# Branch B's second half with GpSimd in a written order, weight sums tile by tile, and early loads of head 0

## The chip, the cores and the metric

The kernel runs on one core of a Trainium2 chip. Its engines are TensorE (PE: matmuls and transposes), VectorE (DVE), ScalarE (ACT), GpSimd (POOL) and SyncE (SP), which here issues every load and store. The metric is the time of one execution in microseconds (us); lower is better. TensorE's clock is granted by a throttle, and the profile lists it as a share of full speed.

## The reference

One encoder block over 1024 tokens of width 1024, with 16 meta tokens in front, in fp32: a norm, one wide projection `w_in`, two attention branches, two gates, and a feed-forward part.

```python
h = rms_norm(concat(meta, x), norm_mix)
proj = h @ w_in                    # qa ka va (512 each) | qb 512, kb vb 128 each | ga gb (1024 each)
# branch A: 4 heads of differential attention over all 1040 keys
s1 = q1 @ k1.T * scale - slope * dist ; s2 = q2 @ k2.T * scale - slope * dist
y_a = rms_norm((softmax(s1) - lam * softmax(s2)) @ v, subln_gain) * 0.8
# branch B: 8 heads (2 groups of 4, one key head each), a window of 128 tokens
# to either side, the meta tokens, and a sink in the divisor
y_b = softmax_with_sink(window(qb @ kb.T) * scale + bias) @ vb
x = x + (sigmoid(ga) * (y_a @ w_branch_a) + sigmoid(gb) * (y_b @ w_branch_b)) @ w_out
x = x + (silu(hn @ w_ff_gate) * (hn @ w_ff_up)) @ w_ff_down      # hn = rms_norm(x, norm_ffn)
out = rms_norm(x, norm_final)[meta dropped]
```

## The kernel before

**Precision.** Each fp32 operand is split into a high and a low half (`split`: ScalarE copies the high half, another engine subtracts it for the low half), and a product is three matmuls: high x high, low x high, high x low. `prep` loads a projection's 1024 x 128 columns (`w_c`), splits them into `wh_c` and `wl_c`, and leaves the low half to GpSimd but for one weight.

**Stages.** 1. The norm, the transposes of the tokens, projections. 2. Branch B's first group (`units_b(0)`) and heads 0 and 1 of branch A's projections. 3. `project_qb(1)`, the second group's queries; then `units_b(1)`, its eight tiles of 128 queries, and the projections of heads 2 and 3 (`project_a(2)`, `project_a(3)`), which send queries, keys and values to memory (`qa_d`, `ka_d`, `va_d`). A scheduler interleaves all of these on TensorE, by what is ready in a model of times; the other engines' order falls out of it. 4. The seam: pools of stage 3 are closed and others opened on their memory; head 0's queries, keys and values are loaded (`load_a`: `aq0_0`, `aq0_1`, `ak0_0`, `ak0_1`, `av0`), and the first gate products run. 5. Branch A, 4 heads x 8 tiles, where TensorE's order is written out by hand, with gate products as filler. 6. The branches' outputs (`ppa`), the merge, `w_out`, the feed-forward part.

**A tile of branch B** (`attend_b`): TensorE makes the scores `bps`, VectorE adds the bias and finds the extreme, ScalarE makes the exponentials, VectorE the reciprocal of the divisor `bdn`, GpSimd multiplies the four heads by it (`bs`) and copies the meta part (`bmd`). `finish`, one tile later, transposes on TensorE (`bpt`), splits (`btr`), multiplies with the values (`bpy`), and stores `yb_d`.

**The gates** are 2 x 8 column blocks, computed with Strassen's scheme of seven products for each 2 x 2 blocking (`order_g`, 56 products, named `pg2_0` for scheme number 2 and block 0). Each is four steps of three 512-column matmuls. Four of the seven need sums of weight blocks: `weight_sums(k)` loads raw blocks `gw` in two halves, makes four sums `gs` on GpSimd, and stores them to `ws_d`, from where `g_load` fetches them. `g_split` splits what was loaded. Products of numbers 1, 6 and 7 are added by VectorE to a kept partial result `gk` fetched again from `g_d`; the others are copied by ScalarE (`gate_stage`) and stored there. The token operand `hT_hi`, `hT_lo` is replaced by sums of tokens (`ts_d`, two loads of 1 MB) when the scheme's number demands it.

**Branch A's filler.** Each tile walks through a string of slots: `s` scores, `g` one gate step, `n` the tail of an earlier pair of tiles, `t` its transposes. Before head 0's first score `G_FIRST` = 28 gate steps run, before each other head `G_HEAD` = 10. `n_gates` is the budget of steps until the last tile: 4 x 56 - 36 = 188, where `HOLD` = 36 are kept for after it. 28, 10 before each of three heads, and five in a tile use it up by tile 26.

**SP** issues transfers in order: one that waits for data holds up those behind it.

Of the kernel before, what the change touches and what calls it, by code (L numbers as in the profile page):

```python
# [9 lines left out]
F32 = mybir.dt.float32  # L10
# [29 lines left out]
SLOTS = "sgsgsngsgsgstntnt"  # L40
SLOTS_LAST = "sgsgsngsgsstntnt"
# [6 lines left out]
HOLD = 36  # L48
# [3 lines left out]
G_FIRST = 28  # L52
# [21 lines left out]
def encoder_block(ctx: ExitStack, tc: tile.TileContext, x, meta, norm_mix, w_in, lq1, lk1, lq2, lk2,  # L74
# [30 lines left out]
    ws_d = {(p, k): dram.tile([P, 4, P], F32, name=f"ws_d{p}_{k}") for p in (5, 3, 6, 7) for k in range(8)}  # L105
# [68 lines left out]
    def prep(col, name, p=None, lo_eng=None):  # L174
        w = wpool.tile([P, DC, P], F32, tag="w", name=f"w_{name}", bufs=2)
        nc.sync.dma_start(w, w_in[:, col:col + P].rearrange("(c p) n -> p c n", p=P))
        p, bufs = (p, 1) if p else (wpool, W_BUFS)
        wh = p.tile([P, DC, P], F32R, tag="wh", name=f"wh_{name}", bufs=bufs)
        wl = p.tile([P, DC, P], F32R, tag="wl", name=f"wl_{name}", bufs=bufs)
        split(wh, wl, w, lo_eng or nc.gpsimd)  # L180
        return wh, wl

    order = [C_KB, C_QB, C_VB]
    for h in range(AH):
        order += [C_QA + h * P, C_VA + h * P, C_KA + h * P]
# [238 lines left out]
    prepped[C_QB + P] = prep(C_QB + P, "qbx", bpool, nc.vector)  # L424
# [129 lines left out]
    def units_b(g, qb, pending=()):  # L554
# [28 lines left out]
    def weight_sums(k):  # L583
        tt = nc.gpsimd.tensor_tensor
        for c in range(0, 4, 2):
            raw = tpool.tile([P, 2, 2, 256], F32, tag="to", name=f"gw_{k}_{c}", bufs=2)
            for kh in range(2):
                nc.sync.dma_start(raw[:, kh], g_weights(k, kh, 0, 256)[:, c:c + 2])
            a11, a21, a12, a22 = (raw[:, i, :, j * P:j * P + P] for i in range(2) for j in range(2))
            s1, s2, s3, s4 = (x[:, i] for x in [tpool.tile([P, 2, 2, P], F32, tag="ta", name=f"gs{j}_{k}_{c}", bufs=3)  # L590
                                                for j in range(2)] for i in range(2))
            tt(s1, a21, a22, ALU.add)
            tt(s3, a11, a21, ALU.subtract)
            tt(s2, s1, a11, ALU.subtract)
            tt(s4, a12, s2, ALU.subtract)
            for i, t in ((5, s1), (7, s3), (6, s2), (3, s4)):
                nc.sync.dma_start(ws_d[i, k][:, c:c + 2], t)
# [5 lines left out]
    def g_load(n, raw=None):  # L603
# [4 lines left out]
        nc.sync.dma_start(raw, ws_d[p, k] if (p, k) in ws_d else g_weights(k, *{2: (1, 0), 1: (0, 0), 4: (1, P)}[p], P))  # L608
# [26 lines left out]
    token_sums(3)  # L635
    qb = new_qb(1)
# [17 lines left out]
    def load_a(h, between=lambda: None):  # L654
        p = apool
        qs, ks = [None, None], [None, None]
        for m in (1, 0):
            q = qs[m] = p.tile([P, S], F32R, tag=f"q{m}", name=f"aq{h}_{m}")
            k = ks[m] = p.tile([P, 2, L], F32R, tag=f"k{m}", name=f"ak{h}_{m}")
            nc.sync.dma_start(f32(q), qa_d[h][m])  # L660
            nc.sync.dma_start(f32(k)[:, 0, :], ka_d[h][m])
            for hl in range(2):
                nc.sync.dma_start(f32(k)[64 - 64 * hl:128 - 64 * hl, 1, :], ka_d[h][m, 64 * hl:64 * hl + 64, :])
            if m:
                between()
        v = p.tile([P, 2, 9, P], F32R, tag="v", name=f"av{h}")
        nc.gpsimd.memset(f32(v)[:, 0, 8, :], 0.0)
        nc.sync.dma_start(f32(v)[:, :, 0:8, :], va_d[h][:, :, 0:8, :])
        nc.sync.dma_start(f32(v)[:2 * NM, 0, 8, :], va_d[h][:2 * NM, 0, 8, :])
        nc.sync.dma_start(f32(v)[2 * NM:3 * NM, 0, 8, :], va_d[h][:NM, 1, 8, :])  # L670
        return qs, ks, v

    project_a(2)
    project_a(3)
    for n in range(2):
        g_load(n, tpool.tile([P, 512], F32, tag="ta", name=f"w_g{n}", bufs=3))
        g_split(n, tpool.tile([P, 2, 4, P], F32R, tag="to", name=f"w_gop{n}", bufs=2))
    g_done[:] = [2, 2]
    ld = load_a(0, lambda: load_sums(5, 0, 1))
    flush_v()  # L680
# [4 lines left out]
    gpool, close_gpool = pool("gpool", "right")  # L685
    g_ahead(0)
# [17 lines left out]

    def gate_steps():
        for n, (p, k) in enumerate(order_g):
            g_ahead(n + 1)
            op, act = g_ready.pop((p, k)), G_ACT[p]
            if p in (2, 5, 1):
                g_bank[k] = pp_bank(f"pg{p}_{k}")  # L710
            ps = g_bank[k]
            for c in range(4):
                for i, (a, b) in enumerate(((0, 0), (0, 1), (1, 0))):
                    nc.tensor.matmul(ps, op[:, a, c], quad(b, *act)[:, c], start=(p in (2, 5, 1) and c == 0 and i == 0),  # L714
                                     stop=(p in (2, 3, 4) and c == 3 and i == 2), skip_group_check=True)
                if c == 3:
                    if p in (1, 6, 7):
                        st = g_kept.pop((p, k))
                        nc.vector.tensor_tensor(st, ps, st, ALU.add)
                    else:  # L720
                        st = gpool.tile([P, 512], F32, tag="g", name="gate_stage", bufs=G_BUFS)
                        nc.scalar.copy(st, ps)  # L722
                    nc.sync.dma_start(g_place(p, k), st)
                    if (p, k) in ((5, 3), (5, 7), (3, 7)):
                        later_p = {(5, 3): 6, (5, 7): 7, (3, 7): 4}[p, k]
                        load_sums(later_p, *G_ACT[later_p])
                yield
# [79 lines left out]
    gates = gate_steps()  # L807

# [639 lines left out]
```

## Time and profile before

| | |
|---|---|
| median of 3 runs | 1499.75 us (1498.25 to 1500.34) |
| the profiled execution | 1498.84 us |
| its span | 1496.9 us |
| TensorE busy in the span | 1439.3 us (96%) |
| GpSimd busy in the span | 667.6 us (45%) |
| VectorE busy in the span | 885.1 us (59%) |
| second group's queries begin | 178.2 us |
| first score of branch A | 365.85 us |
| first product of stage 6 | 670.13 us |

The span is that of the traced instructions in one execution; the execution's own time is 1.9 us longer. A line of the timeline gives the start, the busy time, the engine, the source line, the operation, what it writes and reads, shapes and count, and in square brackets how long the engine stood ahead of it and what released it. A line of the waits gives who waited for what, the sum, the number and the longest. A wait of TensorE counts in the time; one of another engine only where TensorE waits for it in turn.

### The profile page before, as it was taken

How to read it: one execution, taken by the hardware profiler on the slowest of the kernel's cores; microseconds unless marked ns; L12 is line 12 of the kernel's file. 1: busy time of each engine (PE TensorE's matmuls, PEld its weight loads, DVE VectorE, ACT ScalarE, POOL GpSimd, SP SyncE). 2: the span in 40 equal slices, each digit the busy share in tenths (PEclk: the TensorE clock that was granted, in tenths of full speed). 3: DMA queues.
4: the chain of work that ended last, by engine and by line, in shares of the span. 5: the costliest groups of instructions: out<-in, count | busy, mean ns of one | idle time of the engine just before them, and what ended most of it. 6: DMA issues, size and time to landing. Idle time of an engine off the chain costs nothing.

```text
span 1496.9 us, 21310 instructions
## 1 busy us (share of the span) xinstructions
PE 1439.3 (96%) x7279; PEld 1228.5 (82%) x7279; DVE 885.1 (59%) x1610; ACT 679.0 (45%) x1293; POOL 667.6 (45%) x622
## 2 busy tenths in 40 slices
PE   8999989996999999799999999999999999999997
PEld 6999868975989998778888878888888888788886
DVE  7478325541968787833440786655555554778566
ACT  6366425543655555635521573333333333344444
POOL 5599548523343443223732475545554443000344
PEclk9999999998999999999999999999999999999999
DMA  8366778549367747048640345333333333864443
GB/s 238 86 200 210 229 209 257 151 147 284 135 196 249 227 142 248 27 162 260 210 162 22 133 121 162 114 99 104 106 106 106 106 106 106 315 213 134 131 123 141
DMA packets 190204, 242.42 MB, mean 162 GB/s; under 512 B 19520, under 2 KB 117248, under 8 KB 190096
## 3 DMA queue, kind: packets, MB, share of 16 engines
q1 hardware_dynamic: 190096, 241.07, 51.0%
q8 instruction: 57, 0.93, 0.3%
q14 instruction: 51, 0.42, 0.1%
HBM read 157.45 MB, written 77.00 MB: 157 GB/s over the span
## 4 chain that ended last, share of the span: by engine, by line
PE 75%; DMA 7%; POOL 6%; issue 5%; DVE 3%; SPq 2%; ACT 2%; POOLq 0%; ACTq 0%; DVEq 0%
PE pg L1229 26%; PE pg L714 8%; PE pd L1323 8%; PE po L1006 5%; PE ppa L702 4%; PE aps L742 3%; PE pp_va L204 3%; POOL oa L118 3%; PE apy L781 3%; PE pp_qa L204 2%; PE apt L768 2%; PE pp_ka L204 2%; DMA ak<-ka_d 2%; PE bps L318 1%; PE bpt L343 1%
## 5 line engine op out<-in xcount | busy, mean ns | idle before, releaser
L118 POOL TENSOR_TENSOR wop<-wf,wop 128x512 fp32r<-128x512 f32 x128 | 172.4, 1351 | 164.7 <-ACT wop L117 152.3
L1229 PE MATMUL pg<-t,wop 128*128 128x512 f32 x1056 | 242.9, 389 | 0.2 <-POOL wop L118 0.2
L1229 PEld LDWEIGHTS pg<-t,wop 128*128 128x128 f32 x1056 | 198.2, 188 | 41.7 <-POOL wop L118 0.6
L1323 PE MATMUL pd<-ob,oa 128*128 128x512 f32 x924 | 210.2, 389 | 1.7 <-DVE ob L118 1.2
L1323 PEld LDWEIGHTS pd<-ob,oa 128*128 128x128 f32 x924 | 173.3, 188 | 38.4 <-DVE ob L118 1.7
L1229 PE MATMUL pg<-b,wop 128*128 128x512 f32 x792 | 184.0, 390 | 2.3 <-DVE c L1238 2.3
L1229 PEld LDWEIGHTS pg<-b,wop 128*128 128x128 f32 x792 | 148.3, 188 | 33.7 <-issue 2.4
L714 PE MATMUL pg<-hT_hi,gop 128*128 128x512 f32 x432 | 159.9, 399 | 12.9 <-ACT gate_stage L722 12.0
L118 POOL TENSOR_TENSOR gop<-gr,gop 128x512 fp32r<-128x512 f32 x54 | 72.1, 1336 | 151.9 <-ACT gop L117 146.5
L118 POOL TENSOR_TENSOR oa<-ra,oa 128x512 fp32r<-128x512 f32 x33 | 44.0, 1336 | 171.6 <-ACT oa L117 170.2
L117 ACT ACTIVATE wop<-wf 128x512 fp32r<-128x512 f32 x128 | 80.1, 631 | 84.3 <-PE pg L1229 48.5
L714 PEld LDWEIGHTS pg<-hT_hi,gop 128*128 128x128 f32 x432 | 82.1, 190 | 27.4 <-ACT gate_stage L722 12.7
L117 ACT ACTIVATE oa<-ra 128x512 fp32r<-128x512 f32 x77 | 48.7, 632 | 108.2 <-PE pd L1323 53.4
L742 PE MATMUL aps<-ak,aq 128*128 128x392 f32 (+1 forms) x384 | 92.0, 329 | 2.4 <-DVE at L772 0.7
L750 ACT ACTIVATE as<-as,amn 128x1040 f32<-128x1040 f32 x64 | 74.4, 1163 | 37.2 <-DVE amn L745 34.5
L1006 PE MATMUL po<-woh,mT 128*128 128x512 f32 x384 | 88.0, 390 | 0.0
L1064 DVE TENSOR_TENSOR s<-wf,wf 128x512 f32<-128x512 f32 x22 | 25.2, 1145 | 105.9 <-DMA wf<-in_w_ff_gate_dram 58.0
L714 PE MATMUL pg<-hT_lo,gop 128*128 128x512 f32 x216 | 86.0, 398 | 0.0
L1006 PEld LDWEIGHTS po<-woh,mT 128*128 128x128 f32 x384 | 71.9, 188 | 14.8
L742 PEld LDWEIGHTS aps<-ak,aq 128*128 128x128 f32 x384 | 68.7, 188 | 17.6 <-DVE amn L745 2.1
L745 DVE CUSTOM_DVE_ANT_0 as<-aps,dist,far_a 128x392 f32<-128x392 f32 x64 | 39.6, 619 | 51.8 <-PE aps L742 51.1
L320 DVE CUSTOM_DVE_ANT_0 bs<-bps,tbx,nsink 128x432 f32<-128x432 f32 (+1 forms) x64 | 38.1, 623 | 50.4 <-PE bps L318 38.2
(279 smaller groups left out, 3100.8 us busy)
## 6 DMA issues: line engine op xcount, KB each, us to landing
ra<-aop SPq DMA_DIRECT2D x77, 256.0 KB, 2.7
wf<-in_w_ff_gate_dram SPq DMA_DIRECT2D x24, 512.0 KB, 3.9
wf<-in_w_ff_up_dram SPq DMA_DIRECT2D x24, 512.0 KB, 3.8
aop<-as SPq DMA_DIRECT2D x44, 256.0 KB, 2.1
w_c<-in_w_in_dram SPq DMA_DIRECT2D x17, 512.0 KB, 5.8
aop<-c SPq DMA_DIRECT2D x33, 256.0 KB, 2.0
ts_d<-to SPq DMA_DIRECT2D x16, 512.0 KB, 3.9
gw<-in_w_in_dram SPq DMA_DIRECT2D x32, 256.0 KB, 4.2
```

The costliest lines, as they stand in the source:

```text
L117: nc.scalar.activation(hi, src, AF.Copy)
L118: lo_eng.tensor_tensor(lo, src, f32(hi), ALU.subtract)
L204: nc.tensor.matmul(ps[:, :n], a[:, c, :], b[:, c, at:at + n], start=(c == 0 and i == 0), stop=(c == DC - 1 and i == 2))
L702: nc.tensor.matmul(ps, w[:, a, j, :], src(j, b, tk), start=(j == 0 and n == 0), stop=(j == 3 and n == 2))
L714: nc.tensor.matmul(ps, op[:, a, c], quad(b, *act)[:, c], start=(p in (2, 5, 1) and c == 0 and i == 0), stop=(p in (2, 3, 4) and c == 3 and ...
L742: nc.tensor.matmul(ps[:, :n], qs[m][:, t * P:(t + 1) * P], ks[m][:, vv, k0:k0 + n], start=(vv == 0), stop=(vv == 1))
L745: nc.vector.tensor_tensor_reduce(s[m][:, k0:k0 + n], ps[:, :n], far_by, slope, low, ALU.add, ALU.min, mn[:, m, i:i + 1])
L750: nc.scalar.activation(s[m][:, 0:L], s[m][:, 0:L], AF.Exp, bias=low, scale=-1.0, accum_out=dn[:, m:m + 1])
L781: nc.tensor.matmul(py[:, cols], v[:kp, a, k, :], at_[:kp, k, b, :], start=(k == 0 and j == 0), stop=(k == 8))
L1006: nc.tensor.matmul(ps, mT[:, c, a, t * P:(t + 1) * P], wos[q, c][:, b], start=(c == 0 and n == 0), stop=(c == DC - 1 and n == 2))
L1229: nc.tensor.matmul(ps, op[:, x, c, :], b[:, y, c, :], start=(p in (1, 2, 5) and c == 0 and n == 0), stop=(p in (4, 2, 3) and c == 3 and n ...
L1323: nc.tensor.matmul(ps[u], oa[:, a, u * P:(u + 1) * P], ob[:, b, :], start=(p in (1, 2, 5) and j == 0 and k == 0), stop=(p in (2, 3, 4) and ...
```

## The change

It has five parts.

1. The low halves of the query weights of branch B's second group and of all projections of heads 2 and 3 are made by VectorE (`on_vector`), no longer by GpSimd.
2. From `project_qb(1)` to `flush_v()` GpSimd's instructions stand in the order in which they are written (`manual_schedule`). Each tile's `bs` and `bmd` come first, then the tile's two half blocks of weight sums (`sums_of`), whose loads are issued two halves ahead. Two sums go to memory in one store of 256 KB where there were two of 128 KB (`ws_d[k]`).
3. A new pool, `lowpool`, has memory that comes free when branch B's first group is done. `aq0_1`, `ak0_1` and `ak0_0` lie in it and are loaded at the start of stage 3 (`load_a1`, `load_k`). At the seam only `aq0_0` and `av0` are left (`load_a0`).
4. Four gate products (`G_EARLY`) are written ahead of the closing of stage 3's pools, with staging buffers of that stage (`gate_first`). In TensorE's order they stand together behind the last tile of branch B (`bpy_1_7`), as the first products did before, and the next four follow them.
5. `G_FIRST` is 16 steps on top of the 16 of those four products, `HOLD` is 30, and tiles after the first four have four steps of gates and not five. The budget is 4 x 52 - 30 = 178 steps: 16, 10 before each of three heads, and 5 x 4 + 4 x 28 = 132 in the tiles, which is the budget exactly.

The core of the diff:

```diff
-SLOTS = "sgsgsngsgsgstntnt"
-SLOTS_LAST = "sgsgsngsgsstntnt"
+SLOTS = "sgsgsngsgsstntnt"
+SLOTS_MORE = "sgsgsngsgsgstntnt"
-HOLD = 36
+HOLD = 30
+N_MORE = 4
-G_FIRST = 28
+G_FIRST = 16
+G_EARLY = 4
...
-            prepped[col] = prep(col, f"c{col}", lo_eng=nc.vector if col == C_QB else None)
+            prepped[col] = prep(col, f"c{col}", lo_eng=nc.vector if col in on_vector else None)
...
+            extra(t)                                  # in units_b, behind attend_b of tile t
...
+    def weight_sums(n):
+        k, c = n // 2, n % 2 * 2
+        raw, tt = raw_s.pop(n), nc.gpsimd.tensor_tensor
...
+        tt(s1, a21, a22, ALU.add)
+        tt(s2, s1, a11, ALU.subtract)
+        tt(s3, a11, a21, ALU.subtract)
+        tt(s4, a12, s2, ALU.subtract)
+        for j in range(2):
+            nc.sync.dma_start(ws_d[k][:, 2 * j:2 * j + 2, c:c + 2], out[j])
...
+    def load_k(h, m, k):
+        nc.sync.dma_start(f32(k)[:, 0, :], ka_d[h][m])
+        for hl in range(2):
+            nc.sync.dma_start(f32(k)[64 - 64 * hl:128 - 64 * hl, 1, :], ka_d[h][m, 64 * hl:64 * hl + 64, :])
+
+    def load_a1(h):
+        q = [None, lowpool.tile([P, S], F32R, tag="q1", name=f"aq{h}_1", bufs=1)]
+        k = [lowpool.tile([P, 2, L], F32R, tag=f"k{m}", name=f"ak{h}_{m}", bufs=1) for m in range(2)]
+        nc.sync.dma_start(f32(q[1]), qa_d[h][1])
+        load_k(h, 1, k[1])
+        return q, k
...
+    order_pool = tc.manual_schedule(engines={mybir.EngineType.Pool})
+    order_pool.__enter__()
     qb = new_qb(1)
     project_qb(1, qb)
-    for k in range(8):
-        weight_sums(k)
-    units_b(1, qb)
+    for n in range(2):
+        load_s(n)
+    ld = load_a1(0)
+    load_k(0, 0, ld[1][0])
+
+    def sums_of(t):
+        for n in (2 * t, 2 * t + 1):
+            weight_sums(n)
+            if n < 14:
+                load_s(n + 2)
+
+    units_b(1, qb, extra=sums_of)
...
+    for n in range(G_EARLY):
+        g_load(n, tpool.tile([P, 512], F32, tag="ta", name=f"w_g{n}", bufs=3))
+        g_split(n, tpool.tile([P, 2, 4, P], F32R, tag="to", name=f"w_gop{n}", bufs=2))
+    g_done[:] = [G_EARLY, G_EARLY]
+    ld = load_a0(0, *ld)
...
+                        if gpools:
+                            st = gpool.tile([P, 512], F32, tag="g", name="gate_stage", bufs=G_BUFS)
+                        else:
+                            st = f32(stage.tile([P, 2, 512], F32R, tag="qk", name="gate_first", bufs=QK_BUFS))[:, 0]
...
+    gates = gate_steps()
+    for _ in range(4 * G_EARLY):
+        next(gates)
     close_psum1()
     close_tpool()
...
-        for what in SLOTS if n < 3 * NT else SLOTS_LAST:
+        for what in SLOTS_MORE if n < N_MORE else SLOTS:
```

The orders below give in each row the source line, the operation, what it writes and reads with buffer numbers, and shapes.

GpSimd around the first weight sums, before (`bs_0_6` is the normalisation of tile 6 of branch B's first group, `gs0_0_0` and `gs1_0_0` hold the sums of block 0's first half, `gw` the raw blocks):

```order
L592 TENSOR_TENSOR gs0_0_0_2441<-gw_0_0_2438 128x256
L593 TENSOR_TENSOR gs1_0_0_2442<-gw_0_0_2438 128x256
L594 TENSOR_TENSOR gs0_0_0_2441<-gs0_0_0_2441,gw_0_0_2438 128x256
L330 TENSOR_SCALAR bs_0_6_1432<-bs_0_6_1432,bdn_0_6_1434 128x432 x4
L595 TENSOR_TENSOR gs1_0_0_2442<-gw_0_0_2438,gs0_0_0_2441 128x256
L334 COPY bmd0_171<-bs_0_6_1432 128x4x32
L592 TENSOR_TENSOR gs0_0_2_2454<-gw_0_2_2451 128x256
L593 TENSOR_TENSOR gs1_0_2_2455<-gw_0_2_2451 128x256
L594 TENSOR_TENSOR gs0_0_2_2454<-gs0_0_2_2454,gw_0_2_2451 128x256
L595 TENSOR_TENSOR gs1_0_2_2455<-gw_0_2_2451,gs0_0_2_2454 128x256
```

GpSimd at the first tile of the second group in the changed kernel (`bs_1_0` and `bs_1_1` are the normalisations of its tiles 0 and 1):

```order
L338 TENSOR_SCALAR bs_1_0_2434<-bs_1_0_2434,bdn_1_0_2436 128x288 x4
L342 COPY bmd0_150<-bs_1_0_2434 128x4x32
L606 TENSOR_TENSOR gs0_0_0_2467<-gw_0_0_2418 128x256
L607 TENSOR_TENSOR gs0_0_0_2467<-gs0_0_0_2467,gw_0_0_2418 128x256
L608 TENSOR_TENSOR gs1_0_0_2468<-gw_0_0_2418 128x256
L609 TENSOR_TENSOR gs1_0_0_2468<-gw_0_0_2418,gs0_0_0_2467 128x256
L606 TENSOR_TENSOR gs0_0_2_2478<-gw_0_2_2421 128x256
L607 TENSOR_TENSOR gs0_0_2_2478<-gs0_0_2_2478,gw_0_2_2421 128x256
L608 TENSOR_TENSOR gs1_0_2_2479<-gw_0_2_2421 128x256
L609 TENSOR_TENSOR gs1_0_2_2479<-gw_0_2_2421,gs0_0_2_2478 128x256
L338 TENSOR_SCALAR bs_1_1_2489<-bs_1_1_2489,bdn_1_1_2491 128x432 x4
```

The sums no longer run ahead of the tiles nor stand between their parts: two halves follow each normalisation, and the first sums moved from the first group's tiles 6 and 7 to the second group's tile 0.

SP towards the end of the projections, before (`w_g1` is the raw weight of gate product `pg2_1`, `hT_lo` and `hT_hi` the 1 MB token sums, `qa_d3`, `va_d3` and `ka_d3` stores of head 3's projections, `yb_d` stores of branch B):

```order
L608 DMA w_g1_3827<-in_w_in_dram 128x4x128
L535 DMA qa_d3_66<-qk_stage_3581 64x2x512 x2
L357 DMA yb_d2_133<-by1_1_3_2982 64x128 x2
L357 DMA yb_d3_134<-by1_1_3_2982 64x128 x2
L535 DMA qa_d3_66<-qk_stage_3611 64x2x512 x2
L357 DMA yb_d2_133<-by1_1_4_3062 64x128 x2
L357 DMA yb_d3_134<-by1_1_4_3062 64x128 x2
L548 DMA va_d3_74<-va_stage_3723 256x1x512
L540 DMA ka_d3_70<-qk_stage_3742 64x2x272 x2
L568 DMA hT_lo_160<-ts_d5_91 128x4x512
L568 DMA hT_hi_159<-ts_d5_91 128x4x512
```

SP at the same place in the changed kernel (`w_g0` is the raw weight of `pg2_0`, `ws_d7` the store of the last weight sums):

```order
L577 DMA hT_hi_135<-ts_d5_91 128x4x512
L611 DMA ws_d7_102<-gs0_7_2_3132 128x2x256
L577 DMA hT_lo_136<-ts_d5_91 128x4x512
L556 DMA va_d3_74<-va_stage_3709 256x1x512
L622 DMA w_g0_3769<-in_w_in_dram 128x4x128
L611 DMA ws_d7_102<-gs1_7_2_3133 128x2x256
L548 DMA ka_d3_70<-qk_stage_3728 64x2x384 x2
L365 DMA yb_d2_109<-by1_1_6_3180 64x128 x2
L365 DMA yb_d3_110<-by1_1_6_3180 64x128 x2
L556 DMA va_d3_74<-va_stage_3745 64x1x128
L622 DMA w_g1_3774<-in_w_in_dram 128x4x128
```

The gate products' raw weights stood ahead of the two token loads in the queue and stand behind them now.

SP at the seam, before (`gr2_2` to `gr2_5` are raw weights of gate products, `aq0`, `ak0`, `av0` head 0's queries, keys and values, `g_d0` the place of the first product's result):

```order
L608 DMA gr2_2_3858<-in_w_in_dram 128x4x128
L608 DMA gr2_3_3860<-in_w_in_dram 128x4x128
L660 DMA aq0_1_3832<-qa_d0_63 128x1024
L661 DMA ak0_1_3833<-ka_d0_67 128x1040
L663 DMA ak0_1_3833<-ka_d0_67 64x1040 x2
L660 DMA aq0_0_3840<-qa_d0_63 128x1024
L661 DMA ak0_0_3841<-ka_d0_67 128x1040
L663 DMA ak0_0_3841<-ka_d0_67 64x1040 x2
L668 DMA av0_3846<-va_d0_71 128x2x1024
L608 DMA gr2_4_3873<-in_w_in_dram 128x4x128
L723 DMA g_d0_75<-gate_stage_3891 128x512
```

SP at the seam in the changed kernel (`gate_first` are the staging buffers of the first four products):

```order
L622 DMA w_g2_3779<-in_w_in_dram 128x4x128
L622 DMA w_g3_3784<-in_w_in_dram 128x4x128
L666 DMA aq0_0_3789<-qa_d0_63 128x1024
L671 DMA av0_3791<-va_d0_71 128x2x1024
L738 DMA g_d0_75<-gate_first_3823 128x512
L738 DMA g_d2_77<-gate_first_3839 128x512
L672 DMA av0_3791<-va_d0_71 32x128
L673 DMA av0_3791<-va_d0_71 16x128
L738 DMA g_d4_79<-gate_first_3855 128x512
L738 DMA g_d6_81<-gate_first_3871 128x512
L622 DMA gr2_4_3889<-in_w_in_dram 128x4x128
```

Three of head 0's loads with six issues are gone from here, and `gr2_4`, which stood ahead of the first product's store, follows the store of the fourth product, on whose landing it waits, since it lies on memory of the closed staging pool.

At the end of branch A, SP loads branch B's output (`yb_d0` to `yb_d3`) for stage 6. Before, three of these four loads stood ahead of the store of the last kept gate product (`g_d15`); in the changed kernel all four stand behind it, and behind two weight loads, with one more gate store (`g_d13`) among them.

More of the change, by code (lines that the diff above doesn't have):

```diff
@@ L104, in encoder_block @@
     ts_d = {p: dram.tile([P, 2, 4, 512], F32, name=f"ts_d{p}") for p in (5, 6, 7, 4)}
-    ws_d = {(p, k): dram.tile([P, 4, P], F32, name=f"ws_d{p}_{k}") for p in (5, 3, 6, 7) for k in range(8)}
+    ws_d = [dram.tile([P, 4, 4, P], F32, name=f"ws_d{k}") for k in range(8)]
     ya_d = [dram.tile([P, S], F32, name=f"ya_d{h}") for h in range(4)]
@@ L652, in encoder_block @@
         nc.gpsimd.tensor_copy(dist_m[:, t, 0:S - last_k0], dist[:, u0 + last_k0:u0 + S])
[L654 to L671, printed above, removed]
```

127 lines of the change are left out of this document (69 added, 58 removed).

## The prediction

> **What bounds the kernel now.** I read the page's busy times first. TensorE is the bound over the whole span.
>
> ```profile
> PE 1439.3 (96%) x7279; PEld 1228.5 (82%) x7279; DVE 885.1 (59%) x1610; ACT 679.0 (45%) x1293; POOL 667.6 (45%) x622
> ```
>
> The change leaves TensorE's matmuls as they are, so it can only win back time in which TensorE stands or runs at half clock. The busy times of chosen stretches (start and end, length, each engine's busy time, granted clock, DMA share) show where that is.
>
> ```profile
> core 0: us, PE busy (x) PEld busy (x) DVE busy (x) ACT busy (x) POOL busy (x), PEclk, DMA share, GB/s
> 178.20:186.00 7.80, 4.85 (x14) 3.85 (x15) 2.74 (x5) 3.37 (x6) 1.43 (x2) 0.78 0.97 309
> 226.00:234.00 8.00, 6.22 (x22) 5.07 (x23) 2.22 (x6) 5.78 (x12) 7.92 (x11) 0.57 1.01 284
> 232.00:323.00 91.00, 91.00 (x556) 84.66 (x555) 51.03 (x122) 49.24 (x117) 52.73 (x81) 0.99 0.62 187
> 323.00:333.00 10.00, 6.75 (x20) 4.83 (x20) 3.83 (x6) 2.74 (x5) 0.00 (x0) 0.66 0.33 84
> 343.00:360.00 17.00, 5.02 (x14) 3.61 (x13) 0.00 (x0) 3.48 (x6) 4.76 (x4) 0.60 1.04 315
> 178.20:365.90 187.70, 160.78 (x824) 138.87 (x825) 66.26 (x155) 74.83 (x166) 88.52 (x119) 0.92 0.72 214
> 366.00:594.00 228.00, 226.78 (x1373) 204.95 (x1371) 180.72 (x514) 131.96 (x248) 90.88 (x73) 1.00 0.62 200
> 594.00:636.00 42.00, 33.78 (x210) 29.96 (x209) 37.33 (x119) 25.70 (x51) 10.95 (x11) 0.92 0.15 52
> ```
>
> From 178.2 us, where branch B's second group begins, to the first score of branch A at 365.9 us, TensorE stands 187.70 - 160.78 = 26.9 us. The waits of TensorE between 150 and 366 us name three of these gaps, its timeline gives their times:
>
> ```profile
> PE pg L714 <- ACT gate_stage L722: 12.0, 1, 12.0
> PE bpt L343 <- POOL bs L330: 5.5, 1, 5.5
> PE pp_qb L204 <- DVE qk_stage L223: 3.0, 1, 3.0
> ```
>
> ```profile
> 227.34 1.17 PE L343 MATMUL bpt<-ident,bs 128*128 128x128 f32 x4 [5.52 <-POOL bs L330]
> 322.74 0.27 PE L343 MATMUL bpt<-ident,bs 128*128 128x128 f32 x1
> 329.38 0.80 PE L714 MATMUL pg<-hT_hi,w_gop 128*128 128x512 f32 x1 [1.39 <-DVE by L353]
> 355.47 0.80 PE L714 MATMUL pg<-hT_hi,gop 128*128 128x512 f32 x1 [11.98 <-ACT gate_stage L722]
> 359.79 0.39 PE L714 MATMUL pg<-hT_lo,gop 128*128 128x512 f32 x1
> 360.49 0.40 PE L714 MATMUL pg<-hT_lo,gop 128*128 128x512 f32 x1
> ```
>
> After a gap a 512-column matmul takes 0.80 us; at full clock it takes 0.39, and a gate step of three of them starts every 0.70 (359.79 to 360.49). The loss by half clock is (1 - PEclk) times the stretch, less half of the idle time that itself lies at half clock: 1.7 in the first stretch, 3.4 less about 0.6 in the second, 3.4 less 0.7 in the third, and 4.3/2 = 2.1 between 355.47 and 359.79. That is about 9.3 us, so 36 us are lost before the first score: 15.4 up to 234 us (gaps of 3.0, 5.5, and some 2.4 in small ones, 4.5 of clock), 6.0 around 323 to 333, 14.9 from there.
>
> The Trainium skill, page "TensorE: Matmul & The Clock Gate", Part 1, lets the clock fall to half after at least one idle window of about 3.4 us. Here it fell also behind the short gaps ahead of 329.38, so the trace agrees for the long gaps only; by the page the new gaps below would cost some 2 us less clock, and the time would be about 1482.
>
> **GpSimd by hand.** The 5.5 us gap is a queue in the wrong order. VectorE had the divisor ready at 217.00 + 0.18, but GpSimd, in order, stood on a weight sum whose load was late, and normalised (`bs`) only afterwards.
>
> ```profile
> 217.00 0.18 DVE L328 RECIPROCAL bdn<-bdn 128x4 f32<-128x4 f32 x1
> 223.17 0.72 POOL L592 TENSOR_TENSOR gs<-gw 128x256 f32<-128x256 f32 x1 [8.37 <-DMA gw<-in_w_in_dram]
> 226.78 1.47 POOL L330 TENSOR_SCALAR bs<-bs,bdn 128x288 f32<-128x288 f32 x3
> ```
>
> With `bs` ahead of the sums this gap of 5.5 and its 2.8 of clock go. Of the other 7.1 us up to 234 (15.4 - 8.3), which wait on staging copies and their stores, I keep 4: fewer stores stand in the one queue, but 2.6 MB of head 0's keys and queries enter it. Bounds 1 and 8. What is late next in each tile is GpSimd's own cycle:
>
> ```profile
> POOL gs L592 <- DMA gw<-in_w_in_dram: 24.5, 10, 8.4
> L330 POOL TENSOR_SCALAR bs<-bs,bdn 128x432 f32<-128x432 f32 x28 | 17.0, 628 | 12.8 <-DVE bdn L328 12.8
> L595 POOL TENSOR_TENSOR gs<-gw,gs 128x256 f32<-128x256 f32 x16 | 11.8, 740 | 0.3
> ```
>
> Four normalisations and eight operations of sums are 4 x 0.63 + 8 x 0.74 = 8.4 us. TensorE goes from tile 0's transposes (227.34) to tile 7's (322.74) in 95.4 us, 13.6 a tile. So there is room for two waits of 2.6 us on `gw` per tile. Before they were 24.5 / 10 = 2.45 each, but with loads that started late; now a load starts a whole tile ahead. I cost this at nothing. If the cover goes, it is the third rival.
>
> **Low halves on VectorE.** Eight splits leave GpSimd:
>
> ```profile
> L118 POOL TENSOR_TENSOR wl_c<-w_c,wh_c 128x1024 fp32r<-128x1024 f32 x8 | 19.2, 2402 | 2.8 <-PE pp_qa L204 2.1 <-ACT wh_c L117 0.8
> L118 DVE TENSOR_TENSOR wl_qbx<-w_qbx,wh_qbx 128x1024 fp32r<-128x1024 f32 x1 | 1.2, 1214 | 0.0
> ```
>
> GpSimd sheds 19.2 us and VectorE takes 8 x 1.2 = 9.7, beside 51 busy of 91 us: hidden, 0. The Trainium skill, page "GPSIMD Engine Reference", section 1, says that GpSimd shares its SBUF interfaces with VectorE and that they contend when VectorE has two SBUF inputs, which these splits have. By that rule each split could hold GpSimd up for its 1.2 us, one per tile, and 8.4 would become 9.6, still under 13.6. No row of the trace shows such a hold-up: the sums' operation of L593 spans only 722 to 757 ns.
>
> ```profile
> L593 POOL TENSOR_TENSOR gs<-gw x16: 722/738/757, 152.9 to 273.4; 128x256 f32<-128x256 f32 x16
> ```
>
> **The seam.** The 12.0 us gap comes from head 0's loads: the chain of waits runs through a key load and, behind it, a gate product's store.
>
> ```profile
> 334.86 8.91 DMA ak<-ka_d
> ...
> 343.83 10.90 DMA g_d<-gate_stage
> ```
>
> The change takes three of the four key and query loads (2.6 of about 4.2 MB) away from here. But a wait of the same kind stays. The first raw gate weight of the new pool (`gr2_4`) lies over the staging tiles that are now closed, and its load is queued behind the landing of the fourth product's store (`g_d6`). On TensorE `pg2_4` follows `pg2_3` directly, with nothing between. Undisturbed times of these links:
>
> ```profile
> g_d<-gate_stage SPq DMA_DIRECT2D x6, 256.0 KB, 2.0
> gr<-ws_d SPq DMA_DIRECT2D x6, 256.0 KB, 2.6
> L117 ACT ACTIVATE gop<-gr 128x512 fp32r<-128x512 f32 x40 | 25.4, 634 | 27.5 <-PE pg L714 13.6 <-issue 10.3 <-POOL gop L118 3.3
> L722 ACT COPY gate_stage<-pg 128x512 f32<-128x512 f32 x22 | 12.9, 585 | 26.3 <-issue 10.5 <-PE pg L714 7.7 <-DMA g_d<-gate_stage 6.0
> ```
>
> Copy 0.6, store 2.0, load 2.6, high half 0.6, and about 0.4 of issue for each transfer, with some pace lost to the 1 MB load of `av0` beside it: 7.5 us (6.5 to 10), and 2.1 of half clock as after 355.47. So 9.6 takes the place of 14.9.
>
> A second new wait lies ahead of `pg2_0`. Its weight (`w_g0`) is now queued right behind the two 1 MB loads of `hT`, which themselves start only when the last key projection is done, about 7 us ahead of `pg2_0` by the matmuls between. Before, these loads stood behind both gate weights (`w_g0`, `w_g1`) in the queue:
>
> ```profile
> hT_lo<-ts_d SPq DMA_DIRECT2D x1, 1024.0 KB, 5.4
> hT_hi<-ts_d SPq DMA_DIRECT2D x1, 1024.0 KB, 8.3
> ```
>
> 8.3 us for the pair, some 2.5 more for `w_g0` and 0.6 for its high half are 11.4 against 7: a gap of 4 to 5, and with the clock behind it and the small gaps that were there I take 8 in place of 6.0. Bounds 4 and 11.
>
> Before the first score the loss is then 4 + 8 + 9.6 = 21.6 in place of 36.3: **a gain of 14.7** (5 to 23).
>
> **Branch A.** Before, the budget of gate steps ran out at tile 26 of 32, and TensorE stood on VectorE in the last tiles:
>
> ```profile
> PE apt L768 <- DVE as L756: 7.0, 3, 2.6
> ```
>
> That is 42.0 - 33.8 = 8.2 us idle between 594 and 636, and 0.08 x 42 = 3.4 of clock. With four steps in most tiles they last to tile 31. VectorE is next: 180.7 us for 25 tiles are 7.2 a tile; TensorE's tile of five steps is (228 - 3 x 10 x 0.70) / 25 = 8.3, and of four 7.6 (3 x 10 steps stand ahead of the heads). So VectorE nearly fills the new tile, and where adds of 0.68 us fall thicker it is the bound. I take **4 back** of these 11, with ends of -3 (28 tiles 0.1 over) and 8.
>
> **After branch A.** The first product there waits on branch B's output:
>
> ```profile
> 663.48 1.60 SPq L916 DMA_DIRECT2D tb<-yb_d x3
> 665.60 1.15 SPq L916 DMA_DIRECT2D tb<-yb_d x1
> 669.44 1.15 ACT L117 ACTIVATE yb<-tb 128x512 fp32r<-128x512 f32 x2 [0.67 <-DMA tb<-yb_d]
> ```
>
> Before, these loads started 4 to 6 us ahead of that product, and all but hid. Now SP first waits for the last kept product (`g_d15`), with 24 matmuls (5.6 us) left behind it, then issues two weights and the four loads with a further store that waits among them. They come about 3 us later against the gates' end: **3.2 lost** (0 to 6).
>
> **Sum.** 14.7 + 4 - 3.2 = 15.5 us off the profiled execution (1498.84 us, 1.9 over its span) is 1483.3; the runs' median lies 0.9 above it, so **1484**. The terms' ends don't come together; half of their reach gives this case 1474 to 1494.
>
> **Rivals.**
> Seam in time: `w_g0` and the loads behind it land before they are wanted, the tail fills fully and `yb` hides. Then 2 at the seam instead of 8, 8 back in branch A and 0 lost after it: 13 better, 1471. For it: the DMA share was only 0.33 in 323 to 333. Against it: `hT` took 8.3 us even so.
>
> Nothing left over: the gap ahead of `pg2_4` is as long as the old one (the transfers take 10.9 as above and not 2.0), the seam costs 11, VectorE bounds the four-step tiles. Term by term 5 - 3 - 3, about 1499. For it: the DMA share of 1.04 at the old gap. Against it: 2.6 MB are gone from there.
>
> Slower: GpSimd's fixed order. Each tile's normalisation now stands behind two whole sums of the tile before, each waiting for its loads. It decides from a mean wait on `gw` above (13.6 - 8.4) / 2 = 2.6 us, right above the 2.45 of before. At 4.1 each the cycle is 16.6: 3 us x 7 tiles = 21 us of gaps, some with half clock, which less the small gaps that they contain is 23 on top of 1484, so 1507. For it: the longest such wait was 8.4 us and the queue is shared with the early key loads. Against it: the loads start a tile ahead.
>
> **Numbers.** Forecast 0.54, seam in time 0.17, nothing left over 0.13, slower 0.16. The range of 1470 to 1501 holds the first three and leaves the last out. About 0.2% (3 us) is what a measurement of this kernel tells from no change: faster is 0.53 + 0.17 + 0.05, same 0.01 + 0.06, slower 0.16 + 0.02.
>
> **What would show it.** Right: no wait of `bpt` on `bs` at the first tile; the keys' loads before 220 us; a gap of 4 to 5 us ahead of `pg2_0` and of 6.5 to 10 ahead of `pg2_4` with 0.80 us matmuls behind each; the last tiles of branch A without 2.6 us waits of `apt`; `ppa` 3 us late. Wrong: waits of `bpt` on `bs` at most tiles, with GpSimd standing on `gw`; or a first score much later than 354 us: 365.9 less 14.7, and 2.8 more for the four gate steps that now come before it.

## The result, and the profile after

| | before | changed |
|---|---|---|
| median, us | 1500.05 (1498.25 to 1502.3) | 1478.58 (1475.46 to 1479.44) |
| ratio to before | 1 | 0.9852, interval 0.9832 to 0.9872 |
| profiled execution, its span, us | 1498.84, 1496.9 | 1477.96, 1476.2 |
| first score of branch A, us | 365.85 | 353.03 |
| first product of stage 6, us | 670.13 | 648.80 |

The kernel became 21.5 us faster. The forecast was a gain of 15.7 us: 1484, in a range of 1470 to 1501.

TensorE's waits in the changed kernel, first from 150 to 366 us, then from 366 to 680 us (who waited for what, the sum, the number, the longest):

```profile
PE pg L726 <- ACT w_gop L119: 8.4, 2, 5.5
PE pg L726 <- ACT gop L119: 6.7, 1, 6.7
PE bps L326 <- DVE bmn L328: 0.4, 1, 0.4
```

```profile
PE apt L811 <- DVE as L799: 3.5, 3, 2.1
PE ppa L769 <- ACT yb L119: 3.3, 1, 3.3
```

The waits on staging copies, on `bs` and on the 12.0 us store are gone. In their place stand two gaps at the first gate products, one at the first product of the new pool, and one at stage 6. TensorE's timeline gives their times:

```profile
313.01 0.80 PE L726 MATMUL pg<-hT_hi,w_gop 128*128 128x512 f32 x1 [5.45 <-ACT w_gop L119]
323.72 0.79 PE L726 MATMUL pg<-hT_hi,w_gop 128*128 128x512 f32 x1 [2.94 <-ACT w_gop L119]
339.52 0.80 PE L726 MATMUL pg<-hT_hi,gop 128*128 128x512 f32 x1 [6.72 <-ACT gop L119]
353.03 0.52 PE L785 MATMUL aps<-ak,aq 128*128 128x392 f32 x2
616.73 0.86 PE L811 MATMUL apt<-ident,as 128*128 128x128 f32 x4 [2.13 <-DVE as L799]
648.80 31.36 PE L769 MATMUL ppa<-yb,wbhb 128*128 128x512 f32 x123 [3.25 <-ACT yb L119]
```

The two stretches that were at 0.78 and 0.57 of the clock run at full clock without a gap (start and end, length, busy time of the engines from TensorE on, granted clock, DMA share, GB/s):

```profile
178.20:186.00 7.80, 7.80 (x36) 6.32 (x35) 2.55 (x4) 1.27 (x2) 0.00 (x0) 1.00 0.72 212
226.00:234.00 8.00, 8.00 (x56) 7.61 (x56) 5.70 (x15) 5.88 (x13) 5.54 (x8) 1.00 0.75 234
```

GpSimd's waits from 150 to 320 us show what its written order costs and saves:

```profile
POOL bs L338 <- DVE bdn L336: 52.2, 3, 49.0
POOL gs L606 <- DMA gw<-in_w_in_dram: 3.1, 1, 3.1
```

It stands 49 us ahead of the first tile's `bs`, because no sum may go ahead of that; TensorE's list above has no wait on GpSimd. The waits on `gw` after 178 us fell from 24.5 us to 3.1, since each load starts a tile ahead. That is the cover that the prediction named.

The early loads went out sooner than "at the start of stage 3". SP's timeline has the first issue of each of the two key loads in the first group's time, and only the queries behind the start of stage 3 at 176.5 us:

```profile
131.68 0.35 SPq L653 DMA_DIRECT2D ak<-ka_d  x1
160.30 0.58 SPq L653 DMA_DIRECT2D ak<-ka_d  x1
180.81 0.57 SPq L660 DMA_DIRECT2D aq<-qa_d  x1
```

So of the 2.6 MB that were expected to crowd the queue up to 234 us, about 2.1 MB had gone before. The DMA share from 178.2 to 234 us is 0.65; in the kernel before it is 0.81.

### The profile page after: what moved, and what is told of

It reads as the page before. It is cut to its first block, busy times and chain, and to the rows that moved or that the text cites. A ratio compares the mean times of both kernels' runs of the same rounds, so it can differ in the third digit from the quotient of the medians.

```text
span 1476.2 us, 21253 instructions
## 1 busy us (share of the span) xinstructions
PE 1435.2 (97%) x7279; PEld 1226.9 (83%) x7279; DVE 888.0 (60%) x1618; ACT 682.0 (46%) x1293; POOL 650.7 (44%) x614
## 4 chain that ended last, share of the span: by engine, by line
PE 79%; POOL 6%; DVE 5%; issue 4%; DMA 4%; ACT 1%; SPq 1%; POOLq 0%; ACTq 0%; DVEq 0%
PE pg L1271 27%; PE pg L726 9%; PE pd L1365 8%; PE po L1048 6%; PE ppa L769 5%; PE aps L785 4%; PE apy L824 3%; PE pp_qb L211 3%; POOL oa L120 3%; PE pp_va L211 2%; PE pp_qa L211 2%; PE apt L811 2%; PE pp_ka L211 1%; PE bpt L351 1%; PE bps L326 1%
## 5 line engine op out<-in xcount | busy, mean ns | idle before, releaser
L726 PE MATMUL pg<-hT_hi,gop 128*128 128x512 f32 x416 | 154.8, 398 | 6.9 <-ACT gop L119 6.7
L120 POOL TENSOR_TENSOR gop<-gr,gop 128x512 fp32r<-128x512 f32 x52 | 68.6, 1321 | 135.7 <-ACT gop L119 135.6
L726 PEld LDWEIGHTS pg<-hT_hi,gop 128*128 128x128 f32 x416 | 79.1, 190 | 20.1 <-ACT gop L119 7.2
L1106 DVE TENSOR_TENSOR s<-wf,wf 128x512 f32<-128x512 f32 x22 | 18.7, 848 | 107.9 <-DMA wf<-in_w_ff_gate_dram 54.8
L726 PE MATMUL pg<-hT_lo,gop 128*128 128x512 f32 x208 | 82.8, 398 | 0.0
L338 POOL TENSOR_SCALAR bs<-bs,bdn 128x432 f32<-128x432 f32 (+1 forms) x64 | 41.5, 668 | 84.0 <-DVE bdn L336 68.3
```

The costliest lines, as they stand in the source:

```text
L120: lo_eng.tensor_tensor(lo, src, f32(hi), ALU.subtract)
L338: nc.gpsimd.tensor_scalar(st[:, r, :W], st[:, r, :W], dn[:, r:r + 1], 1.0, ALU.mult, ALU.mult)
```

## The experiments

**Branch A's filler alone.** On the kernel before:

```diff
-SLOTS = "sgsgsngsgsgstntnt"
-SLOTS_LAST = "sgsgsngsgsstntnt"
-HOLD = 36
+SLOTS = "sgsgsngsgsstntnt"
+SLOTS_MORE = "sgsgsngsgsgstntnt"     # tiles 0 to 3
+HOLD = 34
```

> The kernel before with the change's gate filler in branch A alone: four gate steps in tiles after the fourth, HOLD 34, so that the budget (190 = 28 + 30 + 132) reaches the last tile. Theory (the gain of 8.5 us between branch A's first score and the gates' end is the filler's, VectorE has room in a four-step tile): 1500 - 8.5 = 1491.5 us, 1489 to 1494; the 2 to 2.6 us waits of apt in the last tiles shrink to one or none, and the gaps of 3.0, 5.5 and 12.0 us before the first score stay. Rival (branch A gains because its keys and its first gate products arrive in better order): 1500 within 2.

Measured: 1490.11 us, ratio 0.9933 (0.991 to 0.9957), about 10 us faster. From the first score (364.5) to stage 6 (660.8) it takes 296.3 us where before it took 304.3. TensorE's waits in branch A:

```profile
PE apt L769 <- DVE as L757: 2.5, 2, 1.8
```

The waits of 7.0 us have shrunk to 2.5. So the filler's part is 8 us by itself, whatever the rest of the change does. The gaps before the first score did not stay as expected: the wait on `bs` is 2.4 us here (5.5 before), the last one 14.3 (12.0). Their sum hardly moved: TensorE stands 25.2 us from 178.2 us to the first score, and 26.9 before. The size of one of these waits is thus no firm figure by itself.

**GpSimd's order.** The `manual_schedule` of GpSimd is taken out of the changed kernel:

```diff
-    order_pool = tc.manual_schedule(engines={mybir.EngineType.Pool})
-    order_pool.__enter__()
...
-    order_pool.__exit__(None, None, None)
```

> The changed kernel with GpSimd ordered by the scheduler again; the early loads, VectorE's low halves and the merged stores stay. Its order puts twelve half blocks of sums ahead of the second group's tile 0 and the raw gate weights w_g0 to w_g3 ahead of the two hT loads. Theory (hand order removes the wait of bpt on bs): a wait of 3 to 10 us with its half clock comes back at the first tiles, while the gaps of 5.5 and 2.9 ahead of pg2_0 and pg2_2 shrink: 1473 to 1486, and the two parts are seen apart in the trace. Rival (the eight low halves on VectorE relieved GpSimd, its order does not matter): no wait of bpt on bs, and with the gaps at pg2_0 smaller 1468 to 1474.

Measured: 1480.01 us, ratio 0.9864 (0.9843 to 0.9885), not to be told from the changed kernel's 0.9852. But the trace differs in both places (TensorE's waits, 150 to 372 us):

```profile
PE pg L723 <- ACT gop L119: 9.2, 1, 9.2
PE pp_qb L211 <- DVE qk_stage L230: 4.4, 1, 4.4
PE bps L326 <- DMA qb<-qk_stage: 1.7, 1, 1.7
PE bpt L351 <- POOL bs L338: 1.6, 1, 1.6
PE bpt L351 <- DVE btr L355: 1.3, 1, 1.3
```

The early waits are back, though that on `bs` only in part (1.6 us, where 3 to 10 were expected), and the two gaps at the first gate products (8.4 us, and their half clock) are gone. The hand order gained at its head what it lost at its tail, where the gate weights were late.

**Low halves on GpSimd.** In the changed kernel:

```diff
-    on_vector = order[on_vector:] + [C_QB]
+    on_vector = [C_QB]
```

> The changed kernel with the eight low halves of weights back on GpSimd, in the hand order. Theory (GpSimd's tile cycle of 8.7 us has room for one split of 2.4 in 13.6): 1478.6 within 3. Rival (the splits were what crowded GpSimd): waits of bpt on bs, or of projections on wl, at several tiles, 1487 to 1494.

Measured: 1504.71 us, ratio 1.0029 (1.0013 to 1.0045): 26 us slower than the changed kernel, more than either theory gave. The busy times from 235 to 290 us, first of the changed kernel, then of this one:

```profile
235.00:290.00 55.00, 54.63 (x328) 49.94 (x327) 33.66 (x81) 30.11 (x73) 41.32 (x60) 1.00 0.86 264
```

```profile
235.00:290.00 55.00, 41.25 (x160) 26.14 (x161) 31.22 (x75) 27.78 (x68) 50.85 (x75) 0.86 0.79 243
```

TensorE ran half as many matmuls. One group of that stretch in the changed kernel, then the same group and the split that ends the stretch in this one:

```profile
L211 PE MATMUL pp_va<-hT_hi,wl_c 128*128 128x384 f32 (+1 forms) x24 | 7.8, 324 | 0.0
```

```profile
L211 PE MATMUL pp_va<-hT_hi,wl_c 128*128 128x384 f32 x3 | 1.7, 578 | 4.2 <-POOL wl_c L120 4.2
285.16 4.66 POOL L120 TENSOR_TENSOR wl_c<-w_c,wh_c 128x1024 fp32r<-128x1024 f32 x2
```

In the written order five splits stand behind the sums of the last tile, so the projections of heads 2 and 3 cannot fill the gaps between branch B's tiles. The tiles then run alone, TensorE waits on the splits of their transposes (`bpy` on `btr`, 8.4 us) and on `bs` (2.1 us), and the clock falls to 0.86. The rival had the splits crowd GpSimd's work on each tile. By the trace they do not stand there but behind the last tile, and it is their place that costs the time.

**The same move on the kernel before.** Eight low halves on VectorE, GpSimd ordered by the scheduler:

```diff
-            prepped[col] = prep(col, f"c{col}", lo_eng=nc.vector if col == C_QB else None)
+            prepped[col] = prep(col, f"c{col}", lo_eng=nc.vector if col in on_vector else None)
```

> The kernel before with one part of the change: the eight low halves on VectorE, GpSimd ordered by the scheduler as before. Theory (the splits crowd nothing there, they matter only where GpSimd's written order would put them behind all sums): 1499.5 within 3, the gap of 12 us ahead of the first score stays. Rival (GpSimd's 19.2 us of splits were what delayed bs and the sums): the waits of bpt and qk go, 1488 to 1494.

Measured: 1509.97 us, ratio 1.0072 (1.0047 to 1.0098), 11 us slower. Both theories fell: the waits of `bpt` stayed, and the gap at the seam grew (TensorE's waits, and SP's queue there):

```profile
PE pg L716 <- ACT gop L117: 20.2, 1, 20.2
PE bpt L345 <- POOL bs L332: 5.3, 2, 5.0
```

```profile
336.34 0.62 SPq L670 DMA_DIRECT2D av<-va_d  x1
339.02 6.03 SPq L610 DMA_DIRECT2D gr<-in_w_in_dram  x3
```

In the kernel before, two raw gate weights went out ahead of head 0's first load:

```profile
332.66 1.14 SPq L608 DMA_DIRECT2D gr<-in_w_in_dram  x2
333.84 0.50 SPq L660 DMA_DIRECT2D aq<-qa_d  x1
```

Here all of them stand behind head 0's queries, keys and values. But the longer gap is not the 11 us: the first score comes only 2 us later than before (367.8 us), since other waits shrank and stage 3 began 1.7 us earlier. From there to stage 6 the kernel takes 311.1 us where before it took 304.3, with two waits that were not there: 3.6 us on a gate's staging copy at 440 us and 2.2 on the last head's keys. A part of the change that is needed in the whole costs 11 us alone. That this comes from the order of SP's queue fits these rows, but no run shows it.

**Head 0's keys at the seam.** In the changed kernel, `lowpool` is closed with branch B's pool, and head 0's tiles lie in `apool`:

```diff
-    ld = load_a1(0)
-    load_k(0, 0, ld[1][0])
...
     close_bpool()
+    close_low()
...
+    ld = load_a1(0)
+    load_k(0, 0, ld[1][0])
     ld = load_a0(0, *ld)
```

> The changed kernel with head 0's aq0_1, ak0_1 and ak0_0 in the pool of branch A again, loaded at the seam, as before; all else as changed. Theory (the old 12 us gap was these 2.6 MB ahead of the gate stores and weights): the gap ahead of pg2_4 grows from 6.7 to 13 to 17 us, 1486 to 1491; nothing changes up to 300 us but some DMA share. Rival (the gap is the chain of store, load and split over closed memory, and the keys hide beside it): 1478.6 to 1481.

Measured: 1486.8 us, ratio 0.991 (0.9887 to 0.9934), 8 us slower than the changed kernel:

```profile
PE pg L726 <- ACT gop L119: 15.6, 1, 15.6
```

The gap ahead of `pg2_4` grows from 6.7 to 15.6 us, as the theory said. Early loading is worth these 8 to 9 us.

**Gate weights in memory of their own.** The first gap has two candidates, the queue and the shared buffers:

```diff
-        g_load(n, tpool.tile([P, 512], F32, tag="ta", name=f"w_g{n}", bufs=3))
+        if n % 2 == 0:
+            w_raw = wpool.tile([P, DC, P], F32, tag="w", name=f"w_g{n}", bufs=2).rearrange("p (a c) n -> p a (c n)", a=2)
+        g_load(n, w_raw[:, n % 2])
```

> The changed kernel with the raw weights of the first four gate products in buffers of the projections' raw weights, no longer in those of the weight sums, so that their loads need not wait for the last sums' stores and stand ahead of the hT loads in the queue. Theory (the gaps of 5.5 ahead of pg2_0 and 2.9 ahead of pg2_2, with some 4.5 us of half clock behind them, are these late loads): both go, 1478.6 - 10 = 1468, 1465 to 1472; the gap ahead of pg2_4 stays at 6 to 9 us. Rival (branch B's last tile sets the start of pg2_0 and the queue at the seam is full): the gaps move behind other waits, 1474 to 1479.

Measured: 1469.95 us, ratio 0.9802 (0.9784 to 0.9819), 9 us faster than the changed kernel. Its waits there:

```profile
PE pg L728 <- ACT gop L119: 10.8, 1, 10.8
PE pg L728 <- POOL w_gop L120: 0.5, 1, 0.5
```

Both gaps are gone, and 4 of the 13 us that they held (8.4, and some 4.5 of half clock) went into the next gap. The edit takes the loads out of the sums' buffers and puts them ahead of `hT` in the queue as well (the last two go out at 281.8 us, `hT` at 298.8), so it does not part the two candidates. The trace of the changed kernel names both. The load of `w_g0` goes out at 301.2 us without a wait, behind the 2 MB of `hT`, and takes 11.0 us to land. For the gap ahead of `pg2_2` the chain of waits has

```profile
303.78 9.16 DMA ws_d<-gs
```

a store of 256 KB of weight sums, also behind `hT`. `w_g1` lies in a buffer of the sums and goes out when this store has landed, and `w_g2` stands behind it in the queue.

**The early stores apart.** The third and fourth early result go to `apool`:

```diff
+                        elif n >= 2:
+                            st = apool.tile([P, 512], F32, tag="gf", name="gate_first", bufs=2)
```

> The changed kernel with the results of the third and fourth early gate product staged in branch A's pool, so that gr2_4's load over the closed staging memory waits for the second's store. Theory (the gap ahead of pg2_4 is the chain copy, store, load, split): it falls from 6.7 to 1 to 4 us, 1472 to 1477. Rival (the load is late by the shared queues at the seam, not by the store): the gap stays at 6 us or more, 1477 to 1480.

Measured: 1471.53 us, ratio 0.9811 (0.9793 to 0.9828), 7 us faster than the changed kernel.

```profile
PE pg L726 <- ACT gop L119: 2.3, 1, 2.3
```

The gap of 6.7 is 2.3, and the clock falls less behind it (0.75 from 334 to 340 us; 0.60 in the changed kernel from 339.5 to 345): the chain over the closed memory was its cause. The time is half a microsecond below the range that the theory gave.

**Both seam edits.** The two edits above in one kernel:

> Both seam edits on the changed kernel, the gate weights in their own memory and the third and fourth result staged apart. Theory: the terms add, 1468 - 4 = 1464, 1460 to 1468, and the first score comes 12 to 16 us earlier than the changed kernel's 353. Rival: one gap takes up what the other gives back, as both hang on the same queue, 1468 to 1474.

Measured: 1469.1 us, ratio 0.98 (0.978 to 0.9821). The terms do not add: the gap ahead of `pg2_4` is 9.5 us, as the rival had it. With the early weights on time, `pg2_4` is wanted earlier, while `aq0_0` and `av0` still stand ahead of its weight in the queue.

**More filler at the end.** `HOLD` 36 for 30 and `G_HEAD` 8 for 10:

> The changed kernel with HOLD 36 for 30 and G_HEAD 8 for 10: six gate steps move from the heads' starts to the end of branch A. Theory (ppa waits 3.3 us since only 24 matmuls stand behind the last kept product): the wait falls under 1 us, 1478.6 - 3 = 1475.5, 1474 to 1477. Rival (eight steps no longer cover the later heads' loads): waits of aps on ak at three heads, 1478 to 1486.

Measured: 1470.67 us, ratio 0.9808 (0.9791 to 0.9825), 8 us faster than the changed kernel and 5 more than expected. The busy times around the end of branch A, of the changed kernel and of this one:

```profile
585.00:649.00 64.00, 58.61 (x340) 52.05 (x339) 34.79 (x93) 27.61 (x51) 20.66 (x16) 0.96 0.33 112
```

```profile
585.00:642.00 57.00, 54.81 (x314) 47.61 (x312) 29.26 (x78) 24.12 (x47) 19.17 (x16) 1.00 0.38 132
```

Besides the wait of stage 6, which fell to 0.7 us, the six steps shortened waits of the last tails; idle time fell from 5.4 to 2.2 us, and with shorter gaps the clock stays at 1.00. Eight steps cover the later heads' loads: there is no wait of `aps` on `ak`.

**All together.** Early weights, six or eight products ahead of the closing, and the filler at the end:

```diff
-G_EARLY = 4
-G_FIRST = 16
-G_HEAD = 10
-HOLD = 30
+G_EARLY = 6          # the other kernel: 8
+G_FIRST = 8          # 0
+G_HEAD = 8
+HOLD = 36
...
+                        elif n >= G_EARLY - 2:
+                            st = apool.tile([P, 512], F32, tag="gf", name="gate_first", bufs=2)
```

> All that helped together: the gate weights in their own memory, six products (not four) ahead of the closing of the pools with the last two staged apart and 8 gate steps (not 16) behind them, HOLD 36 and G_HEAD 8. The one gap left at the seam then stands ahead of pg2_6, 5.6 us later than ahead of pg2_4, when aq0_0 and av0 have landed. Theory (the 9.5 to 10.8 us gap of the two kernels with early weights is the 1.5 MB of aq0_0 and av0 queued ahead of gr2_4): it falls to 3 to 5 us, 1470 - 7 for the gap - 8 for the filler at the end = 1455, 1451 to 1461. Rival (the gap follows the closing of the pools wherever it stands): it stays at 9 to 11, 1461 to 1464.

> The same with eight products ahead of the closing of the pools and none behind them: the first load into the new pool is then wanted inside branch A's first tile. Theory: its wait hides in part beside the first scores, 1452, 1448 to 1460. Rival (tile 0 has no other work for TensorE, and its softmax waits for the same slots): the gap stands in tile 0 with 5 us or more, 1457 to 1464.

Measured: 0.9734 of before (0.971 to 0.9758; 1460.5 us) with six, 0.9753 (0.9727 to 0.9778) with eight. Both beat the changed kernel; the two are not told apart. With six one gap is left, at 6.8 us between the theory's 3 to 5 and the rival's 9 to 11; the queries and values ahead of its weight in the queue, the theory's cause, thus explain only a part of it. With eight it falls apart into several waits around and inside the first tiles, near the rival's case (first fence six, second eight):

```profile
PE pg L728 <- ACT gop L119: 6.8, 1, 6.8
```

```profile
PE pg L728 <- ACT gate_first L741: 2.4, 1, 2.4
PE aps L789 <- DVE amn L792: 2.2, 2, 2.0
```

**The order once more.** The kernel with six early products, GpSimd ordered by the scheduler:

> The kernel with six early products and mended loads, but GpSimd ordered by the scheduler. Theory (the hand order is worth the waits that the scheduler's order brought back between 178 and 290 us: 4.4, 1.7, 1.6, 1.3 and their half clock, 9 to 11 us, which in the changed kernel the hand order's own late gate weights ate up): 1460.5 + 9 = 1469, 1466 to 1473. Rival (with the gate weights in their own memory the order does not matter): 1458 to 1463.

Measured: 1469.98 us, ratio 0.9802 (0.9775 to 0.9829): 9.5 us slower than with the hand order, as the theory had it. The early waits are back, while the gap at the seam is 5.2 us (6.8 with the hand order):

```profile
PE pp_qb L211 <- DVE qk_stage L230: 3.9, 1, 3.9
PE bps L326 <- DMA qb<-qk_stage: 2.5, 1, 2.5
PE bpt L351 <- POOL bs L338: 1.9, 1, 1.9
```

## Why the prediction was right, point by point

The spans differ by 20.7 us. Of these 1.7 lie ahead of 178 us, where the change does nothing on TensorE; the other runs of changed kernels vary there by over 1 us too, and the run with the filler alone, which is the kernel before up to there, begins stage 3 at 175.7 us, so I count it as scatter. From there to the first score TensorE gained 187.7 - 176.5 = 11.2 us (353.03 less 176.5, where its stage 3 begins), and did four gate steps (2.8) more: 14.0. From there to the end of the gates it gained 303.8 - 292.5 = 11.3, 2.8 of them steps that were moved: 8.5. Stage 6 gave back 3.4, 2.8 in its first wait and 0.6 behind it.

- **Before the first score: 14.7 forecast, 14.0 measured.** The sum was right and its parts were not; that they cancel is luck. I kept 4 us of loss up to 234 us, with a lower bound of 1; measured is 0 (TensorE is busy for all of 176.5 to 234.0 us, at full clock). My reason for the 4, head 0's keys in the queue, did not hold: they had gone before 178 us. At the seam I allowed 8 for a gap ahead of `pg2_0`. That gap came, by the mechanism named (5.5 for 4 to 5), but a second one, of 2.9 ahead of `pg2_2`, was not in the step: I saw `w_g0` behind `hT`, not that the weights behind it shared buffers with the sums and waited for their stores. With the clock the two held some 13 us, beyond the bound of 11. The chain ahead of `pg2_4` was as forecast: 6.7 us in the range of 6.5 to 10.
- **GpSimd's order: right in mechanism, and the cover held.** Waits on `gw` fell to 3.1 us in all. Its worth of 9.5 us shows only where the seam is mended; against the scheduler's order it gained nothing in the changed kernel, as the late gate weights that it brings ate it up.
- **Low halves at 0: right as a sum, incomplete as a reason.** I named VectorE's free time as cover. What mattered is that the splits must not stand in GpSimd's written order; left there, they cost 26 us. For that kernel (1504.7) the third rival had the right engine and price (1507), but another mechanism. I also held that no row shows a split holding GpSimd up. The row that I took could not show it, as the splits ran on GpSimd there. In the changed kernel four of them did hold it up, by about 1 us each (rows in the last section); that stayed within the room of a tile, as I had reckoned for this case.
- **Branch A: 4 forecast, 8.5 measured, bound 8.** The term was mis-sized. I held that VectorE nearly fills a tile of four steps and kept 7 of the 11 us of loss. The run with the filler alone gave 8.0, and of the 7.0 us of `apt` waits 3.5 are left in the changed kernel. The tiles are TensorE's: 227.1 busy of 229 us.

```profile
353.00:582.00 229.00, 227.06 (x1387) 205.63 (x1386) 189.94 (x547) 138.47 (x259) 88.21 (x74) 1.00 0.59 195
```

- **Stage 6: 3.2 lost forecast, 3.4 measured,** by the mechanism named.
- **The number.** By spans the forecast of 15.5 falls 5.2 us short: 4.5 in branch A and 1.7 of scatter, less 0.9 in the other two terms.
- **The clock.** Behind 2.94 us at 323.72 a matmul took 0.79 us, behind 6.72 us 0.80, and the granted clock is 0.50 from 323.7 to 330.0 us. So a gap shorter than the window that the Trainium skill gives (page "TensorE: Matmul & The Clock Gate", Part 1) did cost clock again; the measurement decides.

What stays open: how much of the 8 us in stage 3 that the hand order saves is the earlier `bs` and how much the emptier queue; the waits that came back without it name both. That `w_g0` and the store of the sums are late because of `hT` was read from the trace, and was not tried by itself.

## What to carry to other kernels

When an order is written out for one engine, look for what else that engine does in the stretch: work that is emitted late in the program (here the splits, here the gate weights in the sums' buffers) lands behind the whole list, and its price can exceed the gain. Undoing a part in the whole and making it alone gave different signs for the same edit (26 us gained in the whole, 11 lost alone), so a part that is costed at nothing should be tried in both ways. Gaps that hang on one queue do not add: mend the last one first, and look where the next one stands.

## What the runs showed of the hardware

The same split on VectorE took 684 ns in one stretch and 1371 ns in another. The timeline of the changed kernel in the feed-forward part, VectorE and GpSimd, and a group of VectorE from 1300 us on:

```profile
1385.25 1.37 DVE L120 TENSOR_TENSOR ob<-wd_c,ob 128x512 fp32r<-128x512 f32 x1 [0.75 <-ACT ob L119]
1384.77 1.29 POOL L120 TENSOR_TENSOR oa<-ra,oa 128x512 fp32r<-128x512 f32 x1 [1.43 <-ACT oa L119]
L120 DVE TENSOR_TENSOR ob<-wd_e,ob 128x512 fp32r<-128x512 f32 x11 | 7.5, 684 | 0.0
```

VectorE's long ones lie beside a GpSimd operation of 1.29 us, which does not stretch itself and which began 0.48 us earlier; VectorE's ends 0.56 us after it. In stage 3 it is the other way round. There the moved splits, twice as long, kept their time of 1.25 us on average (a group of VectorE, 150 to 320 us), and where one began just ahead of a GpSimd operation, GpSimd's stretched, to 1.66 us, ending 0.60 after the split:

```profile
L120 DVE TENSOR_TENSOR wl_c<-w_c,wh_c 128x1024 fp32r<-128x1024 f32 x8 | 10.0, 1245 | 11.9 <-ACT wh_c L119 11.9
214.50 1.22 DVE L120 TENSOR_TENSOR wl_c<-w_c,wh_c 128x1024 fp32r<-128x1024 f32 x1 [1.82 <-ACT wh_c L119]
214.66 1.66 POOL L607 TENSOR_TENSOR gs<-gs,gw 128x256 f32<-128x256 f32 x1
```

The same stands beside each of the four splits that met GpSimd at work: two sums took 1.66 and 1.73 us, where their median is 0.74, and two normalisations of four operations took 3.41, where others took 2.45. With the splits back on GpSimd (the run "Low halves on GpSimd") none of the 64 sums took more than 0.76 us; those of line 607 there (shortest, median and longest in ns):

```profile
L607 POOL TENSOR_TENSOR gs<-gs,gw x16: 724/731/738, 212.4 to 281.8; 128x256 f32<-128x256 f32 x16
```

So in these rows the later of the two operations waits for the earlier one. The rule of the Trainium skill that the prediction drew on (page "GPSIMD Engine Reference", section 1: the two engines contend when VectorE has two SBUF inputs) agrees with them. For the rows of the feed-forward part no run took the GpSimd operation away.
